# Paged decode attention: the scores of 16 cached pages as one piece on TensorE, the values as another, and new rows' scores with zero-padded keys

## The chip, the cores and the metric

One core of one Trainium2 chip runs the whole program. The metric is the device time of one execution in microseconds (us): the median of the runs of a kernel.

## The reference, cut to what matters

A two-layer decoder step is computed for a prompt (512 rows) and for 8 sample sequences with 4 new rows each. The second layer has latent attention (MLA) with 8 heads. For a sample, each of its 8 x 4 = 32 query rows attends to 4096 cached positions, which lie in 32 pages of 128 positions, and to its own 4 new positions:

```python
s = (einsum('bthc,bsc->bhts', q_lat, ckv)        # 256 latent columns
     + einsum('bthr,bsr->bhts', q_rope, krope)   # 64 rotary columns
     ) * MLA_SCALE
s = where(kpos <= qpos, s, -1e30)
o = einsum('bhts,bsc->bthc', softmax(s), ckv)    # ckv is key and value
```

Around it stand RMS norms, projections, a pooling branch, memory cross-attention, gates and, for each layer, one output projection with a residual add. All is in float32.

## The kernel before, in words

**Stages.** The first 490 us are the first layer, the shared keys and most of the second layer's gates. There a scheduler orders the instructions. After that the order on TensorE (PE) and on SyncE (SP, which issues the loads) is the order in which the code emits them (`tc.manual_schedule`), and the function `weave` decides it. `weave` takes generators ("threads"), keeps a clock of its own, `now`, and always goes on with the thread that is furthest behind its share. A thread yields `(cost, delay)`: the piece that it has just emitted costs `cost` us of PE, and the thread may not go on for `delay` us more; or it yields a condition on which it waits. A piece is never cut, so where a thread yields decides where another's matmuls may come between.

**Threads.** `round_scores` and `round_values` are the cached pages; `gates_late` four late gates (only at the start); `head_inputs` and `heads` the prompt's attention, head by head; `own_scores` the new rows' scores, in one piece; `out_all` the prompt's output projection; `sample_out`, last, combines the samples' parts and makes their output.

**Rounds.** The 32 pages of each sample are taken 16 at a time: 16 rounds `(b, r)`. A round has two halves `ih` of 8 pages. `load_half` loads a half with eight DMAs on SP, four into a tile `a` (576 columns: keys by position, rotary keys, and keys transposed on the host) and four into a tile `b` (320 columns, without the last). Two rounds' tiles exist. The loads of round n+2 are emitted inside `round_values` of round n, since its last reads free the tiles.

- Keys: the pages in `b` are turned on PE, four 128x128 transposes into a bank `tr` (L135), copied to a tile `kt` by ScalarE (ACT, L994) or VectorE (DVE, L996). There are two turns for each half, and three `kt` buffers.
- Scores of a half: 8 matmuls of the latent columns (L1028), then 8 of the rotary ones (L1039), into a half of one bank `ac`. A query block has 32 columns, so the array is used as four tiles of 128 rows by 32 columns, written `128*32` in the profile; a transpose or an ordinary product uses it whole, `128*128`.
- Softmax: maximum (DVE, L1048), exponential (ACT, L1050) into `rt`.
- Values: the exponentials are turned on PE (L135), copied (DVE, L1062), and 16 matmuls (L1067) follow, again with 32 columns. Each matmul of scores and values shows as two in the profile.

A half's scores are emitted as soon as its own two key turns are, so another thread's pieces and the second half's turns stand between the halves. The values have a yield in the middle.

**The new rows' scores** (`own_scores`): for each sample two matmuls over 128 latent rows (L1415) and one over 64 rotary rows (L1418), of 4 columns each. The last one uses a 64-row tile of the array, since `krT_s` holds 64 rows.

**The samples' residual** `x1s` (256 columns) and the constant `jsum` (128 columns) stay in on-chip memory from their making to the end.

Of the kernel before, what the change touches and what calls it, by code (L numbers as in the profile page):

```python
# [7 lines left out]
F32 = mybir.dt.float32  # L8
# [7 lines left out]
P = 128  # L16
D = 1024
KD = 8
SEQ = 512
NB = 8  # L20
NT = 4
# [9 lines left out]
ULEN = PAD + SEQ + NB * (PAD + NT)  # L31
SOFF = PAD + SEQ

C_ID, C_MASK, C_JSUM, C_SEL = 0, 128, 256, 384
C_NCOS, C_NSIN, C_IFIX, C_MOD, C_TMASK, C_ALL = 416, 448, 480, 544, 546, 550


@with_exitstack
def trunk_kernel(ctx: ExitStack, tc: tile.TileContext, A, O):
# [75 lines left out]
    def cst(shape, dt=F32):  # L115
        return const.tile(shape, dt, name=nm("c"))
# [1 line left out]
    def st(n):  # L118
        return small("s", n=n)

    cp = cst([P, C_ALL])
    ident = cp[:, C_ID : C_ID + P]
    cmask = cp[:, C_MASK : C_MASK + P]
    jsum = cp[:, C_JSUM : C_JSUM + P]
    sel = cp[:, C_SEL : C_SEL + NS]
    ncos = cp[:, C_NCOS : C_NCOS + 32]
    nsin = cp[:, C_NSIN : C_NSIN + 32]
# [17 lines left out]
        if k < 2:  # L145
            nc.sync.dma_start(first[k].rearrange("p (k c) -> p k c", k=KD), A["w_in_a"][20 + k])

    nc.sync.dma_start(cp, A["c_pack"])

    def gain(base, k):  # L150
        return gT[:, base + k : base + k + 1]
# [558 lines left out]
    for j in range(4):  # L710
# [4 lines left out]
                transpose(ps[:, k * P : (k + 1) * P], xT[k0 + k][:, j * P : (j + 1) * P])  # L715
            evac(t[:, k0 * P : (k0 + 4) * P], ps)
        nc.gpsimd.dma_start(x1d[j], t)
    x1s = cst([P, 256])
    ps = ps_("tr")
    for fh in range(2):  # L720
        for j in range(4):
# [5 lines left out]
                stop=True,  # L727
            )
    nc.vector.tensor_copy(x1s, ps[:, :256])
    xo.close()  # L730
    px.close()

# [29 lines left out]
        transpose(ps[:NS, f * P : (f + 1) * P], ck[f][:, SEQ:])  # L762
    nc.vector.tensor_copy(ck_nat, ps[:NS, :256])
    ckT_s = cst([P, 2, NS])
    krT_s = cst([64, NS])
    for f in range(2):
        nc.vector.tensor_copy(ckT_s[:, f, :], ck[f][:, SEQ:])
    nc.vector.tensor_copy(krT_s, kr[:64, SEQ:])
    ckx = [split(pc("c", F32R), pc("c", F32R), ck[f][:, :SEQ]) for f in range(2)]
    kkh, kkl = pc("c", F32R), pc("c", F32R)  # L770
    for r in (0, 64):
# [190 lines left out]
    def ps_(tag):  # L962
        return (rb if tag in rb.tags else hb)(tag)

    pro = Pool("pro", "right", kt=(512, 3), rt=(512, 3), os=(256, 2))
    nats = Pool("nats", "right", a=(4 * PGK, 4), b=(4 * PGW, 4))
    stats_m = cst([P, NB])
    stats_s = cst([P, NB])
# [29 lines left out]
    def round_scores():  # L998
        for n, (b, r) in enumerate(rounds):
            nat, kt = [None, None], {}  # L1000

            def turn_keys(ih, k):
                ps = ps_("tr")
                for g in range(4):
                    transpose(ps[:, g * P : (g + 1) * P], nat[ih][1][:, g, k * P : (k + 1) * P])
                x = pro("kt")
                kt_evac(x, ps)
                kt[ih, k] = x.rearrange("p (s c) -> p s c", s=4)
                return 0.44, 0.8

            ss = None
            for ih in range(2):
                if nat[ih] is None:
                    yield lambda: (n, ih) in loaded and loaded[n, ih][1] <= now[0]
                    nat[ih] = loaded[n, ih][0]
                for k in range(2):
                    if (ih, k) not in kt:
                        yield turn_keys(ih, k)
                if ih == 0 and (n, 1) in loaded and loaded[n, 1][1] <= now[0]:
                    nat[1] = loaded[n, 1][0]  # L1020
                    yield turn_keys(1, 0)
                else:
                    yield 0.0, 0.8
                ss = ss or ps_("ac")
                o = ss[:, ih * 256 : (ih + 1) * 256]
                for k in range(2):
                    for j in range(4):
                        nc.tensor.matmul(  # L1028
                            o[j * NS : (j + 1) * NS, :],
                            lhsT=QT[:, k, b, :],  # L1030
                            rhs=(nat[ih][0][:, :, PGW + k * P : PGW + (k + 1) * P] if j < 2 else kt[ih, k])[
                                :, j % 2 * 2 : j % 2 * 2 + 2, :
                            ],
                            start=k == 0,
                            stop=False,
                        )
                for f in range(2):
                    for j in range(4):
                        nc.tensor.matmul(  # L1039
                            o[j * NS : (j + 1) * NS, :].rearrange("p (i f r) -> p f i r", i=2, f=2)[:, f],  # L1040
                            lhsT=Qr[:, b, f, :],
                            rhs=nat[ih][j // 2][:, j % 2 * 2 : j % 2 * 2 + 2, 256:PGW],
                            start=False,
                            stop=f == 1,
                        )
                yield 1.3, 0.0
            nx, sm = st(1), st(1)
            nc.vector.tensor_reduce(out=nx, in_=ss, axis=AX.X, op=ALU.max, negate=True)  # L1048
            e = pro("rt")
            nc.scalar.activation(e, ss, AF.Exp, bias=nx, accum_out=sm)  # L1050
            scored[n] = nat, e, nx, sm, now[0] + 5.0

    def round_values():
        first_part = None
        for n, (b, r) in enumerate(rounds):
            yield lambda: n in scored and scored[n][4] <= now[0]
            nat, e, nx, sm = scored[n][:4]
            ps = ps_("tr")
            for i in range(4):
                transpose(ps[:, i * P : (i + 1) * P], e[:, i * P : (i + 1) * P])  # L1060
            pT = pro("rt")
            nc.vector.tensor_copy(pT, ps)  # L1062
            yield 0.44, 2.0
            po = ps_("ac")
            for i in range(4):
                for j in range(4):
                    nc.tensor.matmul(  # L1067
                        po[j * NS : (j + 1) * NS, :256],
                        lhsT=pT[:, i * P + j * NS : i * P + (j + 1) * NS],
                        rhs=nat[i // 2][j // 2][:, j % 2 * 2 + i % 2, :256],  # L1070
                        start=i == 0,
                        stop=i == 3,
                    )
                if i % 2 and n + 4 // 2 < len(rounds):
                    load_half(n + 4 // 2, i // 2)
                if i == 1:
                    yield 0.86, 0.0
            if r == 0:
                part = pro("os")
                nc.scalar.copy(part, po[:, :256])  # L1080
                first_part = nx, sm
            else:
                nx0, sm0 = first_part
                mn = stats_m[:, b : b + 1]
                nc.vector.tensor_tensor(out=mn, in0=nx0, in1=nx, op=ALU.min)
                w = st(4)
                nc.vector.tensor_tensor(out=w[:, 0:1], in0=mn, in1=nx0, op=ALU.subtract)
                nc.vector.tensor_tensor(out=w[:, 1:2], in0=mn, in1=nx, op=ALU.subtract)
                nc.scalar.activation(w[:, 2:4], w[:, 0:2], AF.Exp)
                sc = stats_s[:, b : b + 1]  # L1090
                nc.vector.tensor_tensor(out=sc, in0=sm0, in1=w[:, 2:3], op=ALU.mult)
                nc.vector.scalar_tensor_tensor(out=sc, in0=sm, scalar=w[:, 3:4], in1=sc, op0=ALU.mult, op1=ALU.add)
                nc.vector.tensor_scalar_mul(part, part, w[:, 2:3])
                nc.vector.scalar_tensor_tensor(
                    out=part, in0=po[:, :256], scalar=w[:, 3:4], in1=part, op0=ALU.mult, op1=ALU.add
                )
                if b < NB - 1:
                    nc.gpsimd.dma_start(ostore[b], part)
                else:
                    parts[b] = part  # L1100
            yield 0.86, 0.0

    def gates_late():
        for f in range(4, 8):
# [236 lines left out]
    def load_rest():  # L1341
# [7 lines left out]
        for j in range(4):  # L1349
# [2 lines left out]
                A["g_final"].rearrange("(f j c) -> j f c", f=2, j=4)[j].unsqueeze(0).broadcast_to([NS, 2, P]),  # L1352
            )
        gains_f.extend([gfin, gfs])

    def out_rows(fh):
        pts = [ps_("oa") for _ in range(4)]
# [51 lines left out]
    def own_scores():  # L1409
# [3 lines left out]
        for b in range(NB):  # L1413
            for k in range(2):
                nc.tensor.matmul(  # L1415
                    sv[:, b, :], lhsT=QT[:, k, b, :], rhs=ckT_s[:, k, b * NT : (b + 1) * NT], start=k == 0, stop=False
                )
            nc.tensor.matmul(  # L1418
                sv[:, b, :], lhsT=Qr[:64, b, 0, :], rhs=krT_s[:, b * NT : (b + 1) * NT], start=False, stop=True
            )  # L1420
        w = pat("qw")
        tail = w[:NS, :NS].rearrange("p (b t) -> p b t", b=NB)
# [19 lines left out]
    weave([rv, rs, out], [rv, rs])  # L1442
    sp_order.__exit__(None, None, None)
    nats.close()
    fin2 = Pool("fin2", "right", x=(D, 4), g=(D, 1), gs=(256, 1))
    cb = Pool("cb", "right", t=(512, 4), o=(1792, 1), c=(96, 3), ws=(D, 5))
    load_rest()

# [109 lines left out]
    def sample_out():  # L1558
# [10 lines left out]
        for fh in range(2):  # L1569
            psm = ps_("ac")  # L1570
            for s, ks in enumerate(order):
# [12 lines left out]
                if s % 2:  # L1584
                    yield 0.88, 0.5
            fs = slice(fh * P, (fh + 1) * P)
            nc.vector.tensor_tensor(out=x1s[:, fs], in0=psm[:, :P], in1=x1s[:, fs], op=ALU.add)
            nc.scalar.activation(pat("wu")[:, :P], x1s[:, fs], AF.Square, accum_out=sss[:, fh : fh + 1])
        sq = st(1)
        nc.vector.tensor_tensor(out=sq, in0=sss[:, 0:1], in1=sss[:, 1:2], op=ALU.add)  # L1590
        yield 0.0, 1.5
        po = ps_("tr")
        nc.tensor.matmul(po[:, 0:1], lhsT=jsum, rhs=sq, start=True, stop=True)
        r = rstd_cols(po[:, 0:1], 1, P, D)
        nc.vector.scalar_tensor_tensor(out=x1s, in0=x1s, scalar=r, in1=gains_f[1], op0=ALU.mult, op1=ALU.mult)
        for j in range(4):
# [70 lines left out]
def _constants():  # L1667
# [18 lines left out]
    for g in range(4):  # L1686
        w = 2 << g
        pack[:, C_IFIX + 16 * g : C_IFIX + 16 * (g + 1)] = w / np.minimum(np.arange(16) + 1, w)
    pack[:, C_MOD] = p % 16
    pack[:, C_MOD + 1] = p % 64  # L1690
    t = np.arange(NS) % NT
    pack[:NS, C_TMASK : C_TMASK + NT] = np.where(np.arange(NT)[None, :] <= t[:, None], 0.0, -1e30)
    return {
# [41 lines left out]
```

## Time and profile before

| | |
|---|---|
| median of 3 runs | 843.52 us (843.01 to 845.77) |
| the profiled execution's own time | 836.92 us |
| its span, first to last instruction | 835.2 us |
| PE busy | 792.8 us (95%) |
| DVE, ACT, POOL (GpSimd) busy | 506.1, 326.9, 262.4 us |
| DMA moved | 158.01 MB, mean 189 GB/s |

The sums below are made against the profiled execution. A matmul's row begins when it starts to stream and ends when its result is out, so successive rows overlap: what a matmul occupies is the distance from its start to the next start. In a timeline row `x2` merges two neighbours. `PEld` are the weight loads. `L1028` is line 1028 of the kernel.

### The profile page before, as it was taken

What the parts mean: (1) busy time and instruction counts of PE and PEld (TensorE: products, weight loads), DVE (VectorE), ACT (ScalarE), POOL (GpSimd) and SP (SyncE); (2) the same over time, 40 slices, a digit from 0 to 9 for tenths busy, and PEclk for the clock granted to TensorE, in tenths of its full rate; (3) what the DMA queues carried; (4) which work ended last, traced back from release to release, by engine and by line L of the source; (5) the groups of instructions that cost most, each with busy time, mean ns of one, the idle gap of its engine ahead of it and who ended that gap; (6) DMA issues with size and microseconds to landing.
All of it is one profiled execution on the core that took longest, in us unless ns stands there. A gap on an engine that the chain in (4) does not pass through costs nothing.

```text
span 835.2 us, 17542 instructions
## 1 busy us (share of the span) xinstructions
PE 792.8 (95%) x6906; PEld 680.8 (82%) x6906; DVE 506.1 (61%) x941; ACT 326.9 (39%) x650; POOL 262.4 (31%) x213
## 2 busy tenths in 40 slices
PE   6999999978999999999999999899999999999995
PEld 6989998978999989877999897776767767677674
DVE  6757666888763435775766653665665577643313
ACT  7453333322343226335433323444543545342212
POOL 0035223434334313411522342642250230055321
PEclk9999999999999999999999999999999999999999
DMA  8356246511233234636625785967978767776642
GB/s 302 98 179 225 76 177 228 158 58 52 68 121 96 77 120 150 206 89 221 227 89 183 260 295 181 366 225 239 300 246 279 262 205 247 261 267 236 215 177 107
DMA packets 82100, 158.01 MB, mean 189 GB/s; under 512 B 9185, under 2 KB 34402, under 8 KB 81762
## 3 DMA queue, kind: packets, MB, share of 16 engines
q1 hardware_dynamic: 77170, 141.22, 50.9%
q0 software_dynamic: 4848, 15.67, 5.2%
q8 instruction: 54, 0.88, 0.4%
q14 instruction: 28, 0.23, 0.1%
HBM read 147.23 MB, written 9.64 MB: 188 GB/s over the span
## 4 chain that ended last, share of the span: by engine, by line
PE 73%; DVE 10%; DMA 8%; issue 3%; ACT 3%; POOL 2%; SPq 1%; POOLq 0%; DVEq 0%; ACTq 0%
PE pa L94 14%; PE pa L96 14%; PE pa L95 14%; PE tr L135 5%; PE ac L1028 3%; PE ac L1067 3%; DVE v L583 2%; DMA o<-ostore 2%; PE oa L94 2%; PE oa L95 2%; DMA b<-in_cache_P 2%; PE oa L96 2%; PE ac L1039 1%; PE ac L389 1%; SPq L985 1%
## 5 line engine op out<-in xcount | busy, mean ns | idle before, releaser
L94 PE MATMUL pa<-h,wh 128*128 128x272 f32 x832 | 239.7, 291 | 4.5 <-DVE g L613 4.5
L96 PE MATMUL pa<-h,wl 128*128 128x272 f32 x832 | 236.9, 290 | 0.6 <-POOL wl L90 0.6
L90 POOL TENSOR_TENSOR wl<-wr,wh 128x1024 fp32r<-128x1024 f32 (+1 forms) x67 | 156.0, 2330 | 234.7 <-ACT wh L89 220.6
L95 PE MATMUL pa<-h,wh 128*128 128x272 f32 x640 | 184.3, 289 | 0.0
L94 PEld LDWEIGHTS pa<-h,wh 128*128 128x128 f32 x832 | 156.9, 189 | 9.3 <-issue 5.8
L96 PEld LDWEIGHTS pa<-h,wl 128*128 128x128 f32 x832 | 155.6, 189 | 2.4 <-POOL wl L90 1.5
L89 ACT CAST wh<-wr 128x1024 fp32r<-128x1024 f32 (+1 forms) x87 | 87.7, 1008 | 168.4 <-issue 66.8
L95 PEld LDWEIGHTS pa<-h,wh 128*128 128x128 f32 x640 | 120.9, 189 | 1.0
L261 DVE SCALAR_TENSOR_TENSOR g<-t,g 128x272 f32<-128x272 f32 x48 | 49.5, 1037 | 15.3 <-ACT t L260 15.3
L95 PE MATMUL pa<-g,wh 128*128 128x272 f32 x192 | 54.5, 288 | 0.1
L260 ACT ACTIVATE t<-g 128x272 f32<-128x272 f32 x48 | 20.3, 428 | 78.6 <-DVE g L247 78.0
L135 PE MATMUL tr<-c,b 128*128 128x128 f32 x256 | 40.0, 277 | 3.0 <-DVE kt L996 1.7
L94 PE MATMUL oa<-wh,c 128*128 128x512 f32 x96 | 39.5, 412 | 0.0
L95 PE MATMUL oa<-wl,c 128*128 128x512 f32 x96 | 38.0, 395 | 0.7 <-POOL wl L90 0.7
L135 PEld LDWEIGHTS tr<-c,b 128*128 128x128 f32 x256 | 29.7, 140 | 9.7 <-issue 3.0
L95 PEld LDWEIGHTS pa<-g,wh 128*128 128x128 f32 x192 | 36.1, 188 | 0.3 <-DVE g L90 0.3
L994 ACT COPY kt<-tr 128x512 f32<-128x512 f32 x43 | 25.3, 589 | 27.0 <-PE tr L135 26.0
L247 DVE SCALAR_TENSOR_TENSOR g<-pa,r 128x272 f32<-128x272 f32 x42 | 18.2, 438 | 28.8 <-PE pa L96 28.8
L1028 PE MATMUL ac<-kt,c 128*32 128x256 f32 x256 | 35.0, 393 | 0.0
L1028 PE MATMUL ac<-a,c 128*32 128x256 f32 x256 | 34.7, 392 | 0.0
L90 DVE TENSOR_TENSOR q<-q,q 128x512 fp32r<-128x512 f32 x16 | 27.2, 1700 | 10.0 <-ACT q L89 9.9
L90 DVE TENSOR_TENSOR wl<-wr,wh 128x1024 fp32r<-128x1024 f32 x20 | 24.5, 1224 | 12.3 <-ACT wh L89 12.2
(380 smaller groups left out, 1813.0 us busy)
## 6 DMA issues: line engine op xcount, KB each, us to landing
a<-in_cache_P SPq DMA_DIRECT2D x128, 288.0 KB, 4.7
b<-in_cache_P SPq DMA_DIRECT2D x128, 160.0 KB, 4.9
wr<-in_w_in_a SPq DMA_DIRECT2D x24, 512.0 KB, 3.6
wr<-in_w_in_b SPq DMA_DIRECT2D x19, 512.0 KB, 3.6
cs<-in_mem_kT SPq DMA_DIRECT2D x16, 512.0 KB, 5.7
wr<-in_w_out_a SPq DMA_DIRECT2D x16, 384.0 KB, 3.1
wr<-in_w_out_b SPq DMA_DIRECT2D x12, 512.0 KB, 6.3
ws<-in_w_out_b SPq DMA_DIRECT2D x12, 512.0 KB, 5.6
```

Source lines behind the costliest of these rows:

```text
L89: nc.scalar.copy(h, src)
L90: (eng or nc.vector).tensor_tensor(out=l, in0=src, in1=fr(h), op=ALU.subtract)
L94: nc.tensor.matmul(out, lhsT=wh, rhs=xh, start=start, stop=False)
L95: nc.tensor.matmul(out, lhsT=wh, rhs=xl, start=False, stop=False)
L96: nc.tensor.matmul(out, lhsT=wl, rhs=xh, start=False, stop=stop)
L135: nc.tensor.transpose(out, in_, ident[:k, :k])
L247: nc.vector.scalar_tensor_tensor(out=out[:, o : o + HALF], in0=ps[:, :HALF], scalar=scale, in1=bc[:, o : o + HALF], op0=ALU.mult, op1=ALU. ...
L260: nc.scalar.activation(th[:, :HALF], z[:, o : o + HALF], AF.Tanh)
L261: nc.vector.scalar_tensor_tensor(out=z[:, o : o + HALF], in0=th[:, :HALF], scalar=1.0, in1=z[:, o : o + HALF], op0=ALU.add, op1=ALU.mult,)
L994: nc.scalar.copy(out, src)
L1028: nc.tensor.matmul(o[j * NS : (j + 1) * NS, :], lhsT=QT[:, k, b, :], rhs=(nat[ih][0][:, :, PGW + k * P : PGW + (k + 1) * P] if j < 2 else ...
L1067: nc.tensor.matmul(po[j * NS : (j + 1) * NS, :256], lhsT=pT[:, i * P + j * NS : i * P + (j + 1) * NS], rhs=nat[i // 2][j // 2][:, j % 2 * ...
```

## The change

- `round_scores` turns the keys of both halves first (four turns, four `kt` buffers) and then emits all 32 matmul rows of a round's scores as one piece of cost 2.6; the branch that turned one key block of the second half early is gone.
- `round_values` emits its 16 matmuls as one piece of cost 1.72.
- `krT_s` gets 128 rows, of which 64 are zero, and the rotary matmul of the new rows reads all 128 rows of `Qr`. Rows 64 to 127 of the chosen queries are zero as well.
- Room for the fourth `kt` buffer: `x1s` is written to DRAM after it is made and read back in `load_rest`, `jsum` is loaded there too, and two unused constant columns go.

```diff
-    pro = Pool("pro", "right", kt=(512, 3), rt=(512, 3), os=(256, 2))
+    pro = Pool("pro", "right", kt=(512, 4), rt=(512, 3), os=(256, 2))
...
-            ss = None
             for ih in range(2):
-                if nat[ih] is None:
-                    yield lambda: (n, ih) in loaded and loaded[n, ih][1] <= now[0]
-                    nat[ih] = loaded[n, ih][0]
+                yield lambda: (n, ih) in loaded and loaded[n, ih][1] <= now[0]
+                nat[ih] = loaded[n, ih][0]
                 for k in range(2):
-                    if (ih, k) not in kt:
-                        yield turn_keys(ih, k)
-                if ih == 0 and (n, 1) in loaded and loaded[n, 1][1] <= now[0]:
-                    nat[1] = loaded[n, 1][0]
-                    yield turn_keys(1, 0)
-                else:
-                    yield 0.0, 0.8
-                ss = ss or ps_("ac")
+                    yield turn_keys(ih, k)
+            ss = ps_("ac")
+            for ih in range(2):
...
-                yield 1.3, 0.0
+            yield 2.6, 0.0
...
-                if i == 1:
-                    yield 0.86, 0.0
...
-            yield 0.86, 0.0
+            yield 1.72, 0.0
...
-    krT_s = cst([64, NS])
+    krT_s = cst([P, NS])
+    nc.gpsimd.memset(krT_s, 0.0)
-    nc.vector.tensor_copy(krT_s, kr[:64, SEQ:])
+    nc.vector.tensor_copy(krT_s[:64], kr[:64, SEQ:])
...
-                sv[:, b, :], lhsT=Qr[:64, b, 0, :], rhs=krT_s[:, b * NT : (b + 1) * NT], start=False, stop=True
+                sv[:, b, :], lhsT=Qr[:, b, 0, :], rhs=krT_s[:, b * NT : (b + 1) * NT], start=False, stop=True
...
-    x1s = cst([P, 256])
+    x1sd = dram.tile([P, 256], F32, name="x1sd")
+    x1s = pt("t", n=256)
...
     nc.vector.tensor_copy(x1s, ps[:, :256])
+    nc.gpsimd.dma_start(x1sd, x1s)
...
+        xs, js = pat("qw", n=256), fin2("js")
+        nc.gpsimd.dma_start(xs, x1sd)
+        nc.gpsimd.dma_start(js, A["c_pack"][:, C_JSUM : C_JSUM + P])
+        gains_f.extend([xs, js])
```

In the program built from each kernel, this is what stands on PE at three places. The names are tiles with their numbers (they differ between the programs); `ac`, `tr`, `hs`, `po` and `pa` are banks of results, `a` and `b` the page tiles, `kt` turned keys, `rt` exponentials, `c` constants and kept queries. Lines after line 34 move by a few: L1028, L1039, L1067, L1415, L1418 and L135 before are L1023, L1034, L1062, L1412, L1415 and L134 now.

PE, round 11, between the scores of its two halves, before:

```order
L1039 MATMUL ac_8727<-b_8361,c_4070 32x2x64 x2
L135 MATMUL tr_8744<-c_79,b_8396 128x128 x4
L94 MATMUL pa_8755<-c_3819,wuh_8590 128x512
L95 MATMUL pa_8755<-c_3820,wuh_8590 128x512
L96 MATMUL pa_8755<-c_3819,wul_8591 128x512
L94 MATMUL pa_8755<-c_3823,wuh_8590 128x512
L95 MATMUL pa_8755<-c_3824,wuh_8590 128x512
L96 MATMUL pa_8755<-c_3823,wul_8591 128x512
L135 MATMUL tr_8766<-c_79,b_8396 128x128 x4
L1028 MATMUL ac_8727<-a_8395,c_4069 32x256 x2
```

and now:

```order
L1034 MATMUL ac_8679<-a_8292,c_4073 32x2x64 x2
L1034 MATMUL ac_8679<-b_8293,c_4073 32x2x64 x2
L1023 MATMUL ac_8679<-a_8327,c_4072 32x256 x2
L1023 MATMUL ac_8679<-kt_8615,c_4072 32x256 x2
L1023 MATMUL ac_8679<-a_8327,c_4072 32x256 x2
```

The second half's key turns and the values' projection (`pa`) have left the gap; they stand elsewhere in the row. From the first scores to the last values there were 44 unbroken runs of 32-column matmuls, and there are 31 now.

PE, the end of the new rows' scores (shapes `32x4`), before:

```order
L1415 MATMUL tr_9550<-c_3814,c_4069 32x4 x2
L1418 MATMUL tr_9550<-c_3815,c_4070 32x4
L1415 MATMUL tr_9550<-c_3814,c_4069 32x4 x2
L1418 MATMUL tr_9550<-c_3815,c_4070 32x4
L1028 MATMUL ac_9353<-a_9169,c_4069 32x256 x2
```

and now:

```order
L1412 MATMUL tr_9595<-c_3816,c_4072 32x4 x2
L1415 MATMUL tr_9595<-c_3817,c_4073 32x4
L1412 MATMUL tr_9595<-c_3816,c_4072 32x4 x2
L1415 MATMUL tr_9595<-c_3817,c_4073 32x4
L1062 MATMUL ac_9626<-a_9076,rt_9530 32x256 x2
```

They were followed by the scores of half a round and are now followed by a round's values.

PE, round 11, from the turn of the exponentials to the values, before:

```order
L135 MATMUL tr_8853<-c_79,rt_8792 128x128 x4
L100 MATMUL po_8794<-p_8815,vx_8199 128x384
L101 MATMUL po_8794<-p_8815,vx_8200 128x384
L102 MATMUL po_8794<-p_8816,vx_8199 128x384
L135 MATMUL hs_8863<-c_79,e_8723 128x128
L135 MATMUL tr_8869<-c_79,b_8680 128x128 x4
L1067 MATMUL ac_8876<-a_8360,rt_8858 32x256 x2
```

and now:

```order
L94 MATMUL pa_8800<-c_3826,wuh_8747 128x512
L95 MATMUL pa_8800<-c_3827,wuh_8747 128x512
L96 MATMUL pa_8800<-c_3826,wul_8748 128x512
L134 MATMUL tr_8811<-c_79,rt_8730 128x128 x4
L1062 MATMUL ac_8818<-a_8292,rt_8816 32x256 x2
```

Nothing stands any more between the turn and the values that read its copy `rt`. Of the 16 rounds this is so in rounds 4 and 11 now, and in none before; in round 8 now seven transposes stand there, in round 15 three products of 384 columns and a transpose.

At the end of the rounds 78 matmuls of the output projection (`oa`) stood ahead of the last values; now the last values stand inside the last head, and the whole output projection comes after them.

More of the change, by code (lines that the diff above doesn't have):

```diff
@@ L32 @@
 SOFF = PAD + SEQ
-C_ID, C_MASK, C_JSUM, C_SEL = 0, 128, 256, 384
-C_NCOS, C_NSIN, C_IFIX, C_MOD, C_TMASK, C_ALL = 416, 448, 480, 544, 546, 550
+C_ID, C_MASK, C_SEL, C_NCOS, C_NSIN, C_IFIX = 0, 128, 256, 288, 320, 352
+C_TMASK, C_HERE, C_JSUM, C_ALL = 416, 420, 420, 548
 @with_exitstack
@@ L119, in st @@
         return small("s", n=n)
-    cp = cst([P, C_ALL])
+    cp = cst([P, C_HERE])
     ident = cp[:, C_ID : C_ID + P]
     cmask = cp[:, C_MASK : C_MASK + P]
-    jsum = cp[:, C_JSUM : C_JSUM + P]
     sel = cp[:, C_SEL : C_SEL + NS]
@@ L146, in trunk_kernel @@
             nc.sync.dma_start(first[k].rearrange("p (k c) -> p k c", k=KD), A["w_in_a"][20 + k])
-    nc.sync.dma_start(cp, A["c_pack"])
+    nc.sync.dma_start(cp, A["c_pack"][:, :C_HERE])
     def gain(base, k):
@@ L1444, in trunk_kernel @@
     nats.close()
-    fin2 = Pool("fin2", "right", x=(D, 4), g=(D, 1), gs=(256, 1))
+    fin2 = Pool("fin2", "right", x=(D, 4), g=(D, 1), gs=(256, 1), js=(P, 1))
     cb = Pool("cb", "right", t=(512, 4), o=(1792, 1), c=(96, 3), ws=(D, 5))
@@ L1586, in sample_out @@
             fs = slice(fh * P, (fh + 1) * P)
+            x1s = gains_f[2]
             nc.vector.tensor_tensor(out=x1s[:, fs], in0=psm[:, :P], in1=x1s[:, fs], op=ALU.add)
@@ L1592, in sample_out @@
         po = ps_("tr")
-        nc.tensor.matmul(po[:, 0:1], lhsT=jsum, rhs=sq, start=True, stop=True)
+        nc.tensor.matmul(po[:, 0:1], lhsT=gains_f[3], rhs=sq, start=True, stop=True)
         r = rstd_cols(po[:, 0:1], 1, P, D)
@@ L1688, in _constants @@
         pack[:, C_IFIX + 16 * g : C_IFIX + 16 * (g + 1)] = w / np.minimum(np.arange(16) + 1, w)
-    pack[:, C_MOD] = p % 16
-    pack[:, C_MOD + 1] = p % 64
     t = np.arange(NS) % NT
```

## Prediction

> **What bounds the kernel now.** I read the page's busy times and its chain first, then the time cut by stage.
>
> ```profile
> span 835.2 us, 17542 instructions
> PE 792.8 (95%) x6906; PEld 680.8 (82%) x6906; DVE 506.1 (61%) x941; ACT 326.9 (39%) x650; POOL 262.4 (31%) x213
> PE 73%; DVE 10%; DMA 8%; issue 3%; ACT 3%; POOL 2%; SPq 1%; POOLq 0%; DVEq 0%; ACTq 0%
> ```
>
> PE is busy 95% of the span and carries 73% of the chain that ended last; no other engine is near. So a change is worth what it takes off PE's row, plus or minus the waits that it leaves there.
>
> ```profile
> 0.00:490.00 490.00, 469.68 (x3717) 436.73 (x3718) 320.28 (x532) 191.80 (x346) 154.15 (x115) 1.00 0.46 152
> 490.00:740.00 250.00, 238.20 (x2559) 181.35 (x2557) 153.07 (x339) 112.56 (x263) 72.80 (x72) 0.99 0.77 259
> 762.00:836.00 74.00, 63.03 (x496) 46.22 (x488) 23.14 (x57) 15.89 (x31) 22.49 (x21) 0.97 0.53 187
> ```
>
> Columns: stretch, length, busy PE, PEld, DVE, ACT, POOL, granted clock, DMA share, GB/s. The change works in the second row, where PE is busy 238.2 of 250 us: at most 11.8 us are waits between matmuls. What else can be won there must lie inside "busy": matmuls that stand further apart than they need. The last row's 11 us of PE idle are mostly the end, after the last product.
>
> **Fewer changes of the array's tiles.** The timeline of PE, where half a round's scores stand between products of the output projection:
>
> ```profile
> 749.52 0.40 PE L96 MATMUL oa<-wh,g 128*128 128x512 f32 x1
> 749.85 0.41 PE L1028 MATMUL ac<-a,c 128*32 128x256 f32 x2
> ...
> 750.09 0.39 PE L1028 MATMUL ac<-a,c 128*32 128x256 f32 x2
> ...
> 750.31 0.39 PE L1028 MATMUL ac<-a,c 128*32 128x256 f32 x2
> ...
> 750.96 0.28 PE L1039 MATMUL ac<-a,c 128*32 128x128 f32 x2
> ...
> 751.07 0.28 PE L1039 MATMUL ac<-a,c 128*32 128x128 f32 x2
> ...
> 751.29 0.50 PE L94 MATMUL oa<-wh,c 128*128 128x512 f32 x1
> 751.63 0.40 PE L95 MATMUL oa<-wl,c 128*128 128x512 f32 x1
> 751.86 0.39 PE L96 MATMUL oa<-wh,g 128*128 128x512 f32 x1
> ```
>
> A product of 512 columns steps by 0.23 (751.63 to 751.86). Going in, the step is 0.33 (749.52 to 749.85), 0.10 more, and the first group takes 0.24 where the next takes 0.22. Going out, 751.07 to 751.29 is 0.22 against a step of 0.11 (750.96 to 751.07), and the first product then takes 0.34, 0.11 more. In and out cost 0.10 + 0.02 + 0.11 + 0.11 = 0.34 us. With transposes as neighbours, round a round's values:
>
> ```profile
> 527.49 0.60 PE L135 MATMUL tr<-c,b 128*128 128x128 f32 x4
> 528.02 0.41 PE L1067 MATMUL ac<-a,rt 128*32 128x256 f32 x2
> ...
> 529.34 0.39 PE L1067 MATMUL ac<-a,rt 128*32 128x256 f32 x2
> ...
> 529.55 0.39 PE L1067 MATMUL ac<-a,rt 128*32 128x256 f32 x2
> ...
> 529.88 0.66 PE L135 MATMUL tr<-c,b 128*128 128x128 f32 x4
> ```
>
> Four transposes at 0.11 from 527.49 end at 527.93, and the tiles start at 528.02: 0.09. Out, 0.33 against a step of 0.21: 0.12, and the transposes take 0.66 where they took 0.60: 0.06. Sum 0.27. All of this shows as busy. The order has 13 runs fewer (44 to 31), nearly all of them the second halves of scores; I take the middle, 0.31: **4.0 us** less, ends 3.5 and 4.4. Merging the values takes nothing by itself: their 16 matmuls stood together already, with nothing between.
>
> **The new rows' scores.** They change tiles twice for each sample, and the clock falls behind them:
>
> ```profile
> 722.98 0.29 PE L1415 MATMUL tr<-c,c 128*32 128x4 f32 x4
> 723.20 0.22 PE L1418 MATMUL tr<-c,c 64*32 64x4 f32 x2
> ...
> 726.11 0.64 PE L1028 MATMUL ac<-a,c 128*32 128x256 f32 x2
> ...
> 728.83 0.98 PE L135 MATMUL hs<-c,e 128*128 128x128 f32 x7
> ```
>
> ```profile
> L1415 PE MATMUL tr<-c,c x32: 172/173/213, 723.0 to 725.8; 128*32 128x4 f32 x32
> ```
>
> ```profile
> 667.37:670.78 3.41, 1.68 (x13) 1.27 (x11) 3.33 (x8) 1.13 (x4) 2.98 (x3) 1.00 0.22 79
> 670.78:674.19 3.41, 3.41 (x42) 2.22 (x40) 2.79 (x6) 1.44 (x5) 1.94 (x3) 1.00 0.51 118
> 721.97:725.39 3.42, 3.42 (x47) 2.89 (x45) 1.87 (x4) 0.78 (x2) 0.55 (x1) 1.00 0.91 286
> 725.39:728.80 3.41, 3.41 (x44) 2.03 (x41) 1.06 (x6) 0.23 (x1) 0.00 (x0) 0.50 1.04 387
> ```
>
> The piece lasts 726.11 - 722.98 = 3.13 us. Four matmuls of one tile span 0.29 of which one is 0.17, so they step by 0.04; 48 of them without a change of tiles take 1.9 us: **1.2 us** less. (By the distance to the next kind, 0.22 for four, 48 take 2.6: the low end is 0.5; the high end 1.6, if a third of the step is still the entry.)
>
> The clock is the larger part. In 725.39:728.80 the granted clock is 0.50, and half a round's scores take 728.83 - 726.11 = 2.72 us where they take 751.29 - 749.85 = 1.44 at full clock: 1.28 us lost. The stretch before it holds 2.4 us of these four-column matmuls and 1.0 us of real streaming. The stretch 667.37:670.78 holds 1.68 us of PE in all and was followed by full clock. With 1.9 us of small matmuls at least 1.5 us of streaming remain in any such stretch, nearer to 1.68 than to 1.0, so I take the slow window as gone: **1.3 us** less, ends 0 and 1.3.
>
> The Trainium skill, "TensorE: Matmul & The Clock Gate" (Part 1), says that the clock falls to half after a window of about 3.4 us in which PE was idle. Here it fell after a window in which PE's rows cover all 3.42 us, so the trace agrees with the length of the window and not with that word. Read literally the page gives no clock gain, and the sum would be 1.3 us smaller.
>
> **Where waits come.** The order puts a round's values right behind the turn of its exponentials in rounds 4 and 11, and nearly so in 8 and 15. What that costs, from a round whose softmax and turn stand free:
>
> ```profile
> 728.97 0.69 DVE L1048 TENSOR_REDUCE s<-ac 128x1 f32<-128x512 f32 x1 [1.34 <-PE ac L1039]
> 730.06 0.69 ACT L1050 ACTIVATE rt<-ac,s 128x512 f32<-128x512 f32 x1
> 730.90 0.66 PE L135 MATMUL tr<-c,rt 128*128 128x128 f32 x4 [1.08 <-ACT rt L1050]
> 731.31 0.47 PE L100 MATMUL po<-p,vx 128*128 128x512 f32 x1
> 731.72 0.68 DVE L1062 COPY rt<-tr 128x512 f32<-128x512 f32 x1
> ```
>
> PE is free at 731.31; the turn's results are out at 731.56 and their copy takes 0.68, so values behind it start at 732.24 at the earliest: 0.93 us of idle PE, twice 1.9. Round 8 has seven transposes there (0.77): 0.2 left. Round 15 has three products of 384 columns and a transpose (about 0.6, by three quarters of 0.23 each): 0.3 left. Together **2.4 us more**, ends 0 (PE would have waited there for something else anyway) and 4.8 (DVE, in order, has another copy first, as it had here: 731.72 is 0.16 after 731.56, and a whole copy of 0.68 is possible). Between scores and turn the shortest case costs what it cost before: 1.0 us of work in round 8 now, 0.9 in round 14 before, which is the wait of 1.08 above.
>
> **Edits at nothing.** The key copies are now needed 16 matmuls after the fourth turn instead of at once, which can only spare waits. The residual's round trip is three more DMA issues on POOL; four like them take 2.14 us (row below), and both reads stand far ahead of their use, under the whole output projection. If that cover went, the samples' last step would wait for one landing of some 5 us, but 150 products of 0.23 us stand on PE behind the samples' last one.
>
> ```profile
> 762.50 2.14 POOL L1344 DMA_DIRECT2D x<-x1d  x4
> SPq L985 <- PE ac L1067: 74.4, 14, 11.0
> a<-in_cache_P SPq DMA_DIRECT2D x128, 288.0 KB, 4.7
> PE tr L135 <- DMA b<-in_cache_P: 0.4, 1, 0.4
> ```
>
> **The sum:** -4.0 - 1.2 - 1.3 + 2.4 = -4.1 us, that is 836.9 to 832.8 for an execution like the profiled one. The runs' median is 6.6 us above that execution; I carry the difference over: 843.5 - 4.1 = **839.4 us**. About 0.3%, 2.5 us, is what a measurement here tells from no change.
>
> **Rivals.**
> - *The waits eat it (no change).* The four places cost 4.8 instead of 2.4 and the slow window stays (1.3): -4.1 + 3.7 = -0.4, 843.1. For it: the order leaves less between dependent pieces in general, and the last head has no filler after its last values. Against: DVE is busy 153 of 250 us, so not every copy queues.
> - *Page loads come late (slower).* SP waits 74.4 us in 14 waits for values to free the tiles (the waits' row above), so loads are issued at the last moment, and a half lands 4.7 us after its last issue. In the new order the second half's key turn of round 5 stands 11.1 us of PE work behind the end of round 3's values (29 transposes 3.2, products 3.0, a round of scores 2.9, a round of values 1.7, changes 0.3); the shortest by the same count before was 12.1. Against: PE waited for loads 0.4 us in all. It decides from 0.5 us in each of 14 rounds: 7.0 - 4.1 = +2.9, 846.4.
> - *More slow windows (no change).* Four key turns per round stand closer together; if transposes did not count for the clock, new windows at 0.50 would follow, each worth 1.3 us: three give 839.4 + 3.9 = 843.3. Against: of the 13 matmuls in 667.37:670.78 nine are transposes, eight of them the two turns below and one from just before, and the clock stayed. The same page (Part 4) says that transposes do not count as PE-busy in the same way; by this rule that stretch should have slowed the clock, and it did not.
>
> ```profile
> 667.97 0.60 PE L135 MATMUL tr<-c,rt 128*128 128x128 f32 x4
> 670.29 0.66 PE L135 MATMUL tr<-c,b 128*128 128x128 f32 x4 [1.73 <-DVE kt L996]
> ```
>
> - *A change of tiles costs nothing that a wait would not refill (the change doesn't do what it says)*: only the new rows' part is left, 843.5 - 2.5 + 2.4 = 843.4. Against: the gaps above stand where nothing waits.
>
> **How the numbers follow.** Forecast 0.60; waits 0.19, clock 0.05, tiles 0.05; loads 0.11. The forecast's own range is 843.5 - 7.3 = 836.2 (all gains at their upper end, no new wait) to 843.5 - 5.3 + 4.8 = 843.0 (gains 4.0 + 1.3). The whole range reaches over the three cases of no change and leaves out the late loads: 835.5 to 844.5, the low end with the 0.5 us by which runs lie under their median. Faster 0.60 (the forecast, less the part of its range above 841.0, and as much of the waits), same 0.29, slower 0.11.
>
> **What would show it.** Right: runs of 32 score rows unbroken at a step of 0.21, the new rows' scores in 1.9 us or less, clock 1.00 behind them, PE's busy time about 6.5 us smaller in all, new idle of 0.9 before the values of rounds 4 and 11. Wrong: waits of PE for `a` or `b` of the cache above 3 us in all, a second 0.50 window after 490 us, or PE as long busy as now.

## The result, and the profile after

The changed kernel is slower: 851.51 us median of 13 runs (846.63 to 857.04) against 840.41 us of the kernel before beside it (836.04 to 846.37). The ratio is 1.0127 (95%: 1.0102 to 1.0152), some 10.7 us. The prediction was 839.4, that is 4.1 us less than the 843.52 on record then, with 844.5 as its upper end. The profiled execution took 852.03 us; its span is 15.1 us longer than the one before, more than the medians differ, because the profiled execution of before was one of the quicker ones.

The page's busy times and its chain:

```profile
span 850.3 us, 17547 instructions
PE 793.8 (93%) x6906; PEld 683.8 (80%) x6906; DVE 501.4 (59%) x941; ACT 327.1 (38%) x650; POOL 262.0 (31%) x217
PE 48%; DMA 10%; DVE 8%; ACT 3%; issue 2%; POOL 1%; SPq 1%; POOLq 0%; ACTq 0%; DVEq 0%
```

PE does the same 6906 matmuls in nearly the same busy time (793.8 to 792.8 us), so the new time is idle PE. (The 48% is not to be set against the 73% of before: the shares here add up to 73%, because this chain can be followed back only to 235.46 us.) To see where PE is idle, I cut both traces at a place that the two orders share, the memory branch's last turn (482.27 before, 484.27 after), at the last values, and at the last product. Columns as in the prediction. Before:

```profile
482.27:762.06 279.79, 267.88 (x2763) 205.53 (x2763) 164.55 (x360) 121.04 (x276) 86.76 (x83) 0.99 0.77 257
762.06:826.10 64.04, 62.53 (x491) 46.22 (x488) 20.72 (x52) 13.72 (x27) 21.66 (x20) 1.00 0.55 195
sum 343.83, PE 330.41 PEld 251.75 DVE 185.27 ACT 134.77 POOL 108.42; mean PE 165.21 PEld 125.88 DVE 92.63 ACT 67.38 POOL 54.21
```

After:

```profile
484.27:750.55 266.28, 245.50 (x2679) 190.51 (x2679) 156.18 (x353) 116.59 (x269) 79.35 (x81) 1.00 0.78 261
750.55:841.00 90.45, 85.00 (x575) 62.99 (x572) 25.46 (x59) 19.02 (x34) 29.27 (x24) 0.96 0.47 167
sum 356.73, PE 330.50 PEld 253.50 DVE 181.64 ACT 135.61 POOL 108.62; mean PE 165.25 PEld 126.75 DVE 90.82 ACT 67.80 POOL 54.31
```

The stretch is 12.9 us longer (356.73 to 343.83), PE is busy as long (330.50 to 330.41), and idle for 26.2 us instead of 13.4. The last values come 11.5 us earlier on the clock (750.55 to 762.06), but with 84 matmuls fewer done: the 78 products of the output projection that stood ahead of them before now stand behind. The rounds end inside the last head, so nothing of the output projection is left to lie beside either, and the end grows from 64 to 90 us.

What PE waited for over that stretch, in the rows that the reading needs, before (releaser: us in total, times, longest):

```profile
PE tr L135 <- DVE kt L996: 1.7, 1, 1.7
PE tr L135 <- ACT rt L1050: 1.6, 2, 1.1
PE tr L1509 <- DMA o<-ostore: 1.1, 1, 1.1
PE ac L1575 <- DMA ws<-in_w_out_b: 0.4, 1, 0.4
PE tr L135 <- DMA b<-in_cache_P: 0.4, 1, 0.4
```

and after:

```profile
PE tr L134 <- ACT rt L1045: 3.7, 4, 1.4
PE tr L1506 <- DMA o<-ostore: 3.3, 1, 3.3
PE ac L1062 <- DVE rt L1057: 2.9, 4, 0.9
PE ac L1572 <- DMA ws<-in_w_out_b: 2.1, 3, 0.7
PE tr L134 <- DMA b<-in_cache_P: 2.0, 4, 0.8
PE po L102 <- DVE p L90: 1.8, 1, 1.8
```

No single wait makes the loss: exponentials (L1045) and their turned copies (L1057) grow from 1.6 to 6.6 us, the loads of the end (`o`, the samples' stored parts, and `ws`, slabs of the output projection's weights) from 1.5 to 5.4, and the last head's turned attention weights `p` come to 1.8.

**An account of both.** The page counts a matmul as busy until its result is out, so a wait swallows part of what a shorter piece saves. I therefore added up starts: a matmul ahead of a wait occupies its columns at the 512-column step (0.233 us), the rest up to the next start is wait. Time lost to the half-speed clock is the length times one minus the granted clock, and what remains is the work. The same 3251 matmuls, first to last start, in profiled executions of before, after and three experiments told below:

| us | before | room only | padding only | one piece, old plan | after |
|---|---|---|---|---|---|
| length | 343.9 | 348.6 | 344.6 | 353.0 | 356.7 |
| waits (number) | 18.5 (24) | 21.5 (26) | 22.1 (26) | 27.8 (35) | 35.3 (42) |
| half-speed clock | 1.7 | 3.4 | 0.0 | 5.1 | 3.4 |
| work | 323.7 | 323.7 | 322.5 | 320.1 | 318.1 |

The work fell by 5.6 us, and the waits rose by 16.8: 12.1 of it up to the last values, 4.7 behind them.

### The profile page after: what moved, and what is told of

It reads as the page before. It is cut to its first block, busy times and chain, and to the rows that moved or that the text cites. A ratio compares the mean times of both kernels' runs of the same rounds, so it can differ in the third digit from the quotient of the medians.

```text
span 850.3 us, 17547 instructions
## 1 busy us (share of the span) xinstructions
PE 793.8 (93%) x6906; PEld 683.8 (80%) x6906; DVE 501.4 (59%) x941; ACT 327.1 (38%) x650; POOL 262.0 (31%) x217
## 4 chain that ended last, share of the span: by engine, by line
PE 48%; DMA 10%; DVE 8%; ACT 3%; issue 2%; POOL 1%; SPq 1%; POOLq 0%; ACTq 0%; DVEq 0%
PE pa L94 8%; PE pa L95 8%; PE pa L96 8%; PE tr L134 4%; PE ac L1062 3%; DMA b<-in_cache_P 2%; PE ac L1023 2%; DMA o<-ostore 2%; DMA ws<-in_w_out_b 2%; PE oa L94 2%; PE oa L95 1%; PE oa L96 1%; PE ac L1034 1%; DMA wr<-in_w_mem_v 1%; DMA a<-in_cache_P 1%
## 5 line engine op out<-in xcount | busy, mean ns | idle before, releaser
L134 PE MATMUL tr<-c,b 128*128 128x128 f32 x256 | 40.7, 277 | 2.9 <-DMA b<-in_cache_P 2.0
L134 PEld LDWEIGHTS tr<-c,b 128*128 128x128 f32 x256 | 30.2, 141 | 10.3 <-DMA b<-in_cache_P 4.6
L996 ACT COPY kt<-tr 128x512 f32<-128x512 f32 x43 | 25.2, 586 | 27.8 <-PE tr L134 26.8
L1023 PE MATMUL ac<-kt,c 128*32 128x256 f32 x256 | 33.8, 382 | 0.5 <-ACT kt L996 0.5
L1062 PE MATMUL ac<-a,rt 128*32 128x256 f32 x256 | 30.8, 382 | 2.9 <-DVE rt L1057 2.9
L1023 PE MATMUL ac<-a,c 128*32 128x256 f32 x256 | 33.4, 382 | 0.0
```

The costliest lines, as they stand in the source:

```text
L134: nc.tensor.transpose(out, in_, ident[:k, :k])
L996: nc.scalar.copy(out, src)
L1023: nc.tensor.matmul(o[j * NS : (j + 1) * NS, :], lhsT=QT[:, k, b, :], rhs=(nat[ih][0][:, :, PGW + k * P : PGW + (k + 1) * P] if j < 2 else ...
L1062: nc.tensor.matmul(po[j * NS : (j + 1) * NS, :256], lhsT=pT[:, i * P + j * NS : i * P + (j + 1) * NS], rhs=nat[i // 2][j // 2][:, j % 2 * ...
```

## The experiments

Ratios are to the kernel before on the same chip. Theory: the change's savings are real, and the loss comes from its order, in the rounds and at the end. Rivals: the memory edits, the values' piece, or the longer pieces themselves. The values' one piece has no run of its own: in the kernel before, that edit alone leaves the order of PE's rows as it is from first to last. In the changed kernel's order it does move some rows, and the third run takes it back there.

**The padding alone.**

```diff
-    krT_s = cst([64, NS])
+    krT_s = cst([P, NS])
+    nc.gpsimd.memset(krT_s, 0.0)
...
-                sv[:, b, :], lhsT=Qr[:64, b, 0, :], rhs=krT_s[:, b * NT : (b + 1) * NT], start=False, stop=True
+                sv[:, b, :], lhsT=Qr[:, b, 0, :], rhs=krT_s[:, b * NT : (b + 1) * NT], start=False, stop=True
```

> The kernel before with the zero-padded key rows alone; the order on PE is unchanged. Theory (the terms of the sum were right, the loss is elsewhere): new rows' scores 1.5 to 1.9 us instead of 3.13, no half-speed window behind them, 1.2 + 1.3 to 1.7 us less, ratio 0.997 (0.996 to 0.998). Rival (a tile change costs nothing that something else would not refill, or the slow window only moves): 1.000.

Measured: 0.9994 (0.9973 to 1.0016). That is nearer to the rival, and the interval reaches into both. Its timeline around the new rows' scores, with the half round behind them:

```profile
724.36 0.29 PE L1416 MATMUL tr<-c,c 128*32 128x4 f32 x4
725.84 0.40 PE L1029 MATMUL ac<-a,c 128*32 128x256 f32 x1
727.29 0.98 PE L135 MATMUL hs<-c,e 128*128 128x128 f32 x7
```

The piece takes 725.84 - 724.36 = 1.48 us instead of 3.13, and the half round 1.45 instead of 2.72. So 2.9 us are gone here. At the last values nothing is left of them: they end 39.1 us behind the start of this piece in both kernels. The waits of PE from this piece to 746 us:

```profile
PE oa L95 <- POOL wl L90: 1.4, 1, 1.4
PE tr L135 <- ACT rt L1051: 1.1, 1, 1.1
PE tr L135 <- DMA b<-in_cache_P: 0.9, 1, 0.9
PE po L100 <- ACT p L89: 0.7, 1, 0.7
```

The same stretch of before has the 1.1 for the exponentials and 0.7 for `wl`, nothing else: 4.1 against 1.8 us. The weight split on POOL, the page load and the head's weights did not become earlier by PE arriving earlier.

**The room alone**: `x1s` by way of DRAM, `jsum` late, four `kt` buffers, old pieces.

> The kernel before with the room for a fourth kt buffer alone: x1s by way of DRAM, jsum loaded late, four kt buffers; scores and values in their old pieces, 64-row keys. The order on PE is the old one but for some 30 rows between 180 and 350 us. Theory (the order from 490 us on makes the loss): ratio 1.000 to 1.002, the first scores at most 1 us later. Rival (the memory edits make the loss: PE was 2 us late at 470 us already, and the small loads get in the way at the end): 1.004 or more, with the first scores some 2 us or more later and a tail that waits.

Measured: 1.002 (1.000 to 1.004). In the account its work is the old one (323.7), as it must be. The first scores came at 502.24 instead of 499.95; but the kernel before with one late move (below) has 502.13 without these edits, so single executions do not tell that part. By the ratio the room costs about 0.2%, at most 0.4%: a small share of the loss.

**The scores' one piece without the values' and the padding.**

```diff
-            yield 1.72, 0.0
+                if i == 1:
+                    yield 0.86, 0.0
+            yield 0.86, 0.0
...
-    krT_s = cst([P, NS])
+    krT_s = cst([64, NS])
...
```

> The changed kernel with the values in their two pieces again and 64-row keys: of the change, the scores as one piece and the room for it. Theory (the scores' one piece makes the loss, by its order: waits in the rounds, and rounds that end before the last head so that the output projection has nothing to lie beside): ratio 1.012 to 1.018, that is the changed kernel's 1.0127 without the padding's 2.5 us, and no product of the output projection ahead of the last values. Rival (the values' one piece has a share in it): below 1.008.

Measured: 1.0168 (1.0134 to 1.0202), and no product of the output projection ahead of the last values. The scores' piece, with its order and its room, makes the loss; of a share of the values there is no sign.

**Rounds that go slower.** One number, in both threads of the rounds:

```diff
-    rs = Thread(round_scores(), 0.0, 1.0, 70.0)
-    rv = Thread(round_values(), 0.0, 1.0, 34.0)
+    rs = Thread(round_scores(), 0.0, 1.06, 70.0)
+    rv = Thread(round_values(), 0.0, 1.06, 34.0)
```

> The changed kernel with one number changed in the weave: rounds get 1.06 instead of 1.0 of the common share, so they go slower beside the heads; the heads end earlier, and some 80 products of the output projection stand ahead of the last values again, as before. Theory (a good part of the loss is made at the end, where 3.3 us of wait for the stored parts and 3.4 us of a half-speed window follow from rounds that end too early): 4 to 8 us less than the changed kernel, ratio to the kernel before 1.003 to 1.008, and no wait of 3 us behind the last values. Rival (the waits inside the rounds make it): ratio 1.011 or more, PE idle from the first scores to the last values about 20 us as in the changed kernel.

Measured: 1.005 (1.003 to 1.007), 844.24 us: 6 to 7 us back by this alone. 66 products stand ahead of the last values again, the end is 68.0 us long, and the wait for `o` is not among its waits. What is left is mostly in the rounds: PE idle 16.8 us from first scores to last values, against 11.9 before and 20.8 in the changed kernel. The new waits are others:

```profile
PE po L100 <- ACT p L89: 3.1, 1, 3.1
PE pa L94 <- DVE q L1199: 3.0, 7, 0.9
PE ac L1062 <- DVE rt L1057: 1.9, 3, 0.8
PE tr L134 <- ACT rt L1045: 1.4, 1, 1.4
```

**The stored parts first.** In the changed kernel `o` is issued at 753.88, behind five slabs, and lands 18.0 us later. SP's queue there:

```profile
746.31 7.33 SPq L1319 DMA_DIRECT2D ws<-in_w_out_b  x5
753.88 0.43 SPq L1559 DMA_DIRECT2D o<-ostore  x1
754.42 10.54 SPq L1564 DMA_DIRECT2D vx<-in_w_v_up  x2
```

and the clock behind the wait, in stretches of 3.4 us:

```profile
768.60:772.00 3.40, 0.10 (x5) 0.08 (x8) 0.00 (x0) 0.00 (x0) 0.00 (x0) 1.00 1.04 388
772.00:775.40 3.40, 3.40 (x32) 0.68 (x32) 0.00 (x0) 0.00 (x0) 0.00 (x0) 0.56 0.61 232
775.40:778.80 3.40, 3.40 (x12) 2.55 (x9) 0.69 (x1) 0.22 (x1) 0.00 (x0) 0.50 0.04 16
```

PE is idle for one such stretch with the DMA engines full (1.04, 388 GB/s), and then runs at half speed for two. The Trainium skill, "DMA: Bandwidth & Descriptors" (Two DMAs through the same engine are not ordered), says that within one queue of one DMA engine descriptors start in order; the 18.0 us behind five slabs agree.

```diff
-        here = [slab(cb("ws"), *todo.pop(0)) for _ in range(5)]
         o = cb("o").rearrange("p (b c) -> p b c", b=NB - 1)
         nc.sync.dma_start(o, ostore.rearrange("b p c -> p b c"))
+        here = [slab(cb("ws"), *todo.pop(0)) for _ in range(5)]
```

> The changed kernel with one move: the load of the samples' stored parts (o) is issued ahead of the five ws slabs instead of behind them. Theory (at the end, o lands 18 us after its issue because 2.5 MB of ws stand before it; PE waits 3.3 us for it, and two half-speed windows of 3.4 us in all follow that idle): the wait goes, the windows with it, 3.3 to 6.7 us less than the changed kernel, ratio to the kernel before 1.005 to 1.009. Rival (all these loads share one full DMA, so something else is late next: the slabs, x or vx): 1.010 to 1.013, with the wait before another load at the same place. Second rival (the wait goes, but the windows come anyway): 1.008 to 1.010.

Measured: 1.0083 (1.0056 to 1.011), in the theory's range and at the edge of the second rival's. The wait for `o` and the two half-speed stretches behind it are gone. Part of it comes back 20 us later, in a wait for another load as the first rival had it, with one half-speed stretch behind it:

```profile
PE ac L1572 <- DMA ws<-in_w_out_b: 3.1, 2, 2.4
```

Two more half-speed stretches stand in the rounds of this execution (from 579.2 and from 746.5 us), so it lost 5.1 us to the clock from the first cut to the last product, where the changed kernel's lost 3.4. Over the runs the median loss is 10.6 us against 11.0. So the move took the wait away; that it took the half-speed time away is not shown, and the second rival stands in that.

**One piece in the old plan.** Costs and delays as before, so the weave decides as before; the first half's scores are only emitted with the second half's. Against the kernel with the room alone:

```diff
-                ss = ss or ps_("ac")
-                o = ss[:, ih * 256 : (ih + 1) * 256]
+                if ih == 0:
+                    yield 1.3, 0.0
+                    continue
+                ss = ps_("ac")
+                for hh in range(2):
+                    o = ss[:, hh * 256 : (hh + 1) * 256]
...
                 yield 1.3, 0.0
```

> The scores as one piece without a new plan: the pieces keep the costs, delays and yields of the kernel before, but the first half's scores are emitted with the second half's, in its place. So 13 unbroken runs of 32-column matmuls fewer, as in the change, and everything else stands where it stood before, the output projection's 78 products ahead of the last values included. Room for the fourth kt buffer as in the change; 64-row keys, values in two pieces. Theory (fewer changes of tiles gain 1 to 3 us, the loss comes from the re-planned order): ratio 0.998 to 1.001, that is the room's 1.002 less 0.1 to 0.4%. Rival (one piece of scores makes waits wherever it stands, since the products that lay between the halves covered the key copies and the loads): 1.005 or more, PE idle from first scores to last values 17 us or more. The prediction's full 4 us would give 0.997.

Measured: 1.0068 (1.0037 to 1.0099). The theory is too low, the rival holds (PE is idle for 17.5 us from first scores to last values): even in the old plan the longer piece costs. The work fell by 3.6 us against the room alone (323.7 to 320.1, with 13 runs fewer: 0.28 each), and the waits rose by 6.3 and ate it. From the memory branch's last turn to the last values PE waited most for these:

```profile
PE tr L134 <- ACT rt L1054: 2.8, 2, 1.7
PE tr L134 <- DMA b<-in_cache_P: 1.7, 3, 1.2
PE tr L134 <- DVE kt L997: 1.7, 1, 1.7
PE pa L94 <- DVE q L1210: 1.5, 3, 0.8
```

The exponentials' wait was 1.6 with the room alone. All other products stand in the same order in both kernels. So the scores of a first half had lain as filler between dependent steps of heads and rounds; gathered into the second half's place, they are missing there.

**The same with the padding.**

> The same with the zero-padded key rows. Theory (the padding is worth about 1.7 us in its place and up to 1.7 us of clock, but what follows waits for loads and weight splits, so little comes through): 0.000 to 0.002 less than without it, ratio 0.997 to 1.000. Rival (the padding comes through whole): 0.003 to 0.004 less.

Measured: 1.0101 (1.0065 to 1.0136), neither, though the interval overlaps that of the run without the padding. The runs' granted clocks name the reason in part: span times one minus clock, median over runs, is 15.3 us here and 11.8 without the padding. Without that loss it is 1.7 us quicker than its twin, as much as the new rows' scores gain by their rows. Why half-speed stretches came more often stays open.

**Padding and stored parts first, on the kernel before.** The diffs of the padding and of the stored parts, as above.

> The kernel before with the padding and with the load of the stored parts ahead of the ws slabs: scores and values in their old pieces. Theory (o's late landing costs 1.1 us there too, and the place has idle time that can bring a half-speed window): ratio 0.9994 of the padding alone less 0.001 to 0.002, that is 0.997 to 0.998. Rival (the slabs are late instead): 0.999 to 1.001.

Measured: 0.9969 (0.9946 to 0.9992), 838.58 us: it beats both kernels, by 0.3% against the kernel before, as expected. PE is idle for 0.5 us from the last values to the last product.

**The stored parts first, alone.**

> The kernel before with the one move at the end alone: o's load ahead of the five ws slabs; 64-row keys. It parts the two edits of the run with the padding and this move (0.9969). Theory (what that run gained is the move: no wait of 1.1 us at the end, and fewer half-speed windows behind it): ratio 0.996 to 0.998. Rival (the padding is needed for it, because its own gain only comes through where nothing waits behind it): 0.999 to 1.001.

Measured: 0.9984 (0.9965 to 1.0003). That lies between the two ranges, and the interval reaches into both. The two edits are not parted: each may have about half of the 0.3%.

**A longer way from scores to turn**, with the slower rounds and `o` first:

```diff
-            scored[n] = nat, e, nx, sm, now[0] + 5.0
+            scored[n] = nat, e, nx, sm, now[0] + 6.5
```

> The changed kernel with rounds at 1.06 of the common share, o's load ahead of the slabs, and a delay of 6.5 instead of 5.0 between a round's scores and the turn of its exponentials, so that the weave lays more work of other threads between them. Unbroken runs of 32-column matmuls as in the change. Theory (the waits that the change brought into the rounds are short distances behind the pieces, now twice as long): waits of PE for exponentials and their turned copies fall from 6.6 us in the changed kernel to under 2.5, ratio 0.998 to 1.003 against 1.005 with the rounds' share alone. Rival (other work is only moved there, and is missing elsewhere; loads come late, since tiles are freed later): 1.004 or more, as many us of waits under other names.

Measured: 1.008 (1.0054 to 1.0107); the theory falls, the rival holds:

```profile
PE po L102 <- DVE p L90: 4.5, 2, 4.2
PE pa L94 <- DVE q L1199: 3.4, 6, 0.8
PE ac L1062 <- DVE rt L1057: 2.9, 4, 0.9
PE hs L1250 <- POOL qr L1217: 2.3, 1, 2.3
PE tr L134 <- ACT rt L1045: 0.3, 1, 0.3
```

Against the slower rounds alone, the wait for exponentials falls from 1.4 to 0.3, that for their copies grows from 1.9 to 2.9, and the heads wait more: 5.3 us for `p` instead of 3.7, 2.3 for `qr` instead of 0.9. In this trial work laid between one pair of steps was missing at another. The delay was not run without the move of `o`.

**One piece in the old plan, stored parts first.**

> The scores as one piece in the old plan (ratio 1.0068) with o's load ahead of the ws slabs, so that the end is as in the kernel before with that move (0.9984). Theory (13 runs fewer save 3.6 us of PE work, the waits behind the longer pieces give about 4 back in the rounds, and the rest of the 1.0068 is the end's wait for o, 2.1 us, with the half-speed windows behind it): ratio 1.000 to 1.004. Rival (the rounds alone make the loss: waits and half-speed windows there): 1.005 or more with no wait for o.

Measured: 1.0025 (0.9999 to 1.005), as the theory said. Against 0.9984 with that move alone, the scores' piece with its room costs 0.4% in the rounds; against 1.0068, the end gave another 0.4%; in both cases the two intervals overlap. The account says the same of the piece: work 320.0 and waits 25.9 us here, 324.0 and 18.0 with that move alone.

## Why the prediction was wrong

- *Fewer changes of tiles, -4.0:* right. 3.6 measured in the old plan, 0.28 for each run fewer against 0.31.
- *New rows' scores, -1.2:* right or a little low: 1.2 in the account, 3.13 to 1.48 by the rows. *The slow window behind them, -1.3:* it went in its place, as forecast. In the runs, though, padding took nothing off the clock: 8.4 us lost in the median with and without it. A window gone from one profile is not a window gone from the runs.
- *Values behind the turn, +2.4:* 0.78 (rounds 4 and 11), 0.88 (round 13) and 0.44 (round 15) are the 2.9 us of L1057 above, with round 8 at nothing. The size was right; round 13 was not on the list.
- *The step that failed is the rest of the waits, set at nothing.* "Between scores and turn the shortest case costs what it cost before" was wrong: 1.6 us in two places became 3.7 in four. In all, waits rose by 16.8 us where the sum had 2.4. I had looked for places where two dependent pieces touch, and counted the work between them as if everything else kept its distance. The old-plan run shows it apart from the new order: the halves themselves were the filler, 3.6 us saved and 6.3 waited. "The key copies ... can only spare waits" looked at one of many dependent pairs.
- *The end was not in the sum at all.* "150 products of 0.23 us stand on PE behind the samples' last one" was said of the residual's cover. The order had already told that all 288 products of the output projection now follow the last values, where 78 stood ahead of them; I read it for one load only, and not for what the loads `o` and `ws` then collide with. One number in the weave brought 6 to 7 us of the loss back.
- *The rivals:* waits ate it, but not where the first one put them, and 16.8 us against its 4.8; the late loads, the only slower one, were 2.0 us and not 7. New half-speed stretches came (3.4 us lost behind the wait for `o`), for idle time, not for transposes as that rival had it.
- *"PE's busy time about 6.5 us smaller":* it was the same, and this did not mean that the savings were missing. 18 more waits, each with a matmul that counts to the end of its result (4.0 us in all), and 1.7 us more of half-speed clock hide them.

The loss can be read as steps from one kernel to the next, each known only to some 0.2 to 0.4% either way. The room makes 1.002, the one piece in the old plan 1.0068, the new order without the padding 1.0168, and with the padding and the values' one piece it is the changed kernel's 1.0127. The new order is the largest step, about 1.0%, and its interval lies apart from that of the old plan. One share in the weave gives 0.8% back. The longer piece makes 0.5% with the late `o` behind it and some 0.2% with `o` first. With the one piece, the late `o` and what follows it are worth 0.4% in either plan; that lies within these steps. How the single waits in the rounds follow from the plan was not taken further.

## What to carry to other kernels

Where an engine is 95% busy in an interleaved order, as here, a piece that is cut in two can also be filler for other chains: before joining halves, list what stood between each dependent pair and what will stand there now, for every chain and not just for the joined one. Look first at where a long thread ends in the new order, since work without a partner and loads that all start together sit there. And read a saving from starts, not from busy time, when the number of waits changes.

## What the runs showed of the hardware that was not expected

- The half-speed clock makes much of the spread from run to run. Over the changed kernel's runs the span rises by about 1.0 us for each us that the granted clock lost (0.991 at 844.8 us, 0.981 at 855.3 us); over the runs of the kernel before beside the experiments it rises by 0.6 to 0.8. The profiled execution of before had lost 5 us where its runs lose 8 to 10 in the median: that is most of the 3 to 4 us by which it was quicker than they.
- Behind 3.3 us of idle PE the clock stayed at half for two stretches, though PE's rows cover all of the first (3.40 of 3.40). The Trainium skill, "TensorE: Matmul & The Clock Gate" (Part 1), has an idle window of about 3.4 us before half speed, and the trace agrees at this place; it has full speed after one busy window or more, and here it took two. Elsewhere PE was not idle throughout. In the run with the stored parts first these stretches stand next to each other in pairs:

```profile
575.80:579.20 3.40, 1.32 (x16) 0.84 (x20) 2.60 (x6) 2.02 (x5) 0.00 (x0) 1.00 0.53 190
579.20:582.60 3.40, 3.40 (x30) 1.94 (x23) 0.00 (x0) 0.37 (x1) 0.00 (x0) 0.51 0.51 162
743.10:746.50 3.40, 1.54 (x10) 1.04 (x10) 3.26 (x7) 1.25 (x5) 2.15 (x2) 1.00 0.55 183
746.50:749.90 3.40, 3.40 (x26) 1.85 (x28) 1.31 (x3) 0.40 (x2) 0.00 (x0) 0.50 0.96 329
790.90:794.30 3.40, 0.69 (x20) 0.42 (x23) 0.00 (x0) 0.00 (x0) 0.00 (x0) 1.00 1.03 380
794.30:797.70 3.40, 3.40 (x22) 2.38 (x22) 0.00 (x0) 0.00 (x0) 0.00 (x0) 0.50 0.73 269
```

Stretches with 1.32, 1.54 and 0.69 us of PE were each followed by half speed, and each time by one such stretch only. The stretch with 1.68 us that the prediction shows was followed by full speed. What exactly is counted as idle no run here shows.
